# Attention in a two-layer decoder: the rotated queries' high and low parts stacked on the 128 rows of one tile, and the position queries projected before the plain ones

## The chip, the cores and the metric

The kernel runs on one core of a Trainium2 chip. The number that counts is the device time of one execution, in microseconds. TensorE (PE in the profile) multiplies matrices and writes to PSUM; its weight loads have a track of their own, PEld. VectorE is DVE, ScalarE is ACT, GpSimd is POOL, and SyncE (SP) issues most of the transfers from memory.

## The reference

Two layers over 256 positions of width 2048. Layer 0 is a gated short convolution and a squared-ReLU MLP; layer 1 is a latent attention and the same kind of MLP. Each sub-layer ends in a residual sum and a layer norm. The change lies in the attention. Cut to what matters:

```python
def apply_rope(x, cos, sin):
    x1, x2 = xf[..., :half], xf[..., half:]
    out = jnp.concatenate([x1 * cos - x2 * sin, x2 * cos + x1 * sin], axis=-1)

q = (rms_norm(x @ w_dq, q_norm_g) @ w_uq).reshape(bsz, seq, 16, 128 + 64)
q_nope, q_pe = q[..., :128], apply_rope(q[..., 128:], cos, sin)
s = (einsum("bqhd,bkhd->bhqk", qn, k_nope) + einsum("bqhr,bkr->bhqk", qp, k_pe)) * scale
p = softmax(where(mask, s, -inf))
```

There are 16 heads. A head's score is the sum of a plain product over 128 features and a position product over 64 rotated features; the rotated key k_pe is one for all heads.

## The kernel before

Activations lie with features on the 128 partitions and the 256 tokens along the free axis. To get nearly float32 accuracy from TensorE's faster type float32r, most operands are kept as a pair: a high part (the value rounded to float32r, made by ACT) and a low part (the rest, made by DVE with a subtraction); `split` makes both (L137), L139 being its ACT half and L140 its DVE half. A product of two such pairs takes three float32r matmuls: high by high, high by low, low by high. Weights stream from memory as units of 128x1024 floats into a ring of `raw` buffers, and each unit is split; `take` (L229) hands out the next units in the order of the list `stream` (L84 to L111) and prepares units ahead of their use.

In the attention the 16 heads are worked in four groups of four. `project(g, box)` (L1064) is a generator that makes the operands of one group: four key products (`ps_k`), four plain query products (`ps_q`), two position query products (`ps_p`, each for two heads, 64 rows per head), and two value products (`ps_v`). Each item ends in a `yield`. Group 0 is projected alone; after that the projections of group g are interleaved, three items at a time, with the attention steps of group g-1. `together(s)` (L1138) runs, in this order, the last part of head s-3, the middle part of head s-2 and the first part of head s. The first part of `attend` (L1098) makes the scores S and their softmax, the middle part transposes the probabilities (`tp`), the last part multiplies them with the values (`po`).

The scores are made in two spans, queries 0 to 127 against the first 128 keys and queries 128 to 255 against all 256 keys. The operands of the scores are plain float32 here: the plain product is L1107, the position product L1108. The position query tile holds two heads, 64 rows each, and `kpe` holds the rotated key twice, once with zeros in the lower 64 rows and once with zeros in the upper, so that a product over 128 rows takes only one head:

```python
nc.tensor.matmul(S[:, at:at + n], qn[:, tok], kn[:, :n], start=True, stop=False)
nc.tensor.matmul(S[:, at:at + n], qp[:, tok], kp[:, :n], start=False, stop=True)
```

`rope` (L983) rotates: a product with the cosines (L987), products with the sines in pieces of 32 rows that land on the rows 32 further up or down (L990, four for 128 rows), and a sum (L991).

Each engine runs its instructions in its own fixed order. That order is made when the program is built, by a scheduler that keeps dependences between instructions; a change in one place can so move instructions of neighbouring work.

Of the kernel before, what the change touches and what calls it, by code (L numbers as in the profile page):

```python
# [10 lines left out]
F32 = mybir.dt.float32  # L11
F32R = mybir.dt.float32r
AF = mybir.ActivationFunctionType
ALU = mybir.AluOpType
# [42 lines left out]
def trunk(ctx: ExitStack, tc: tile.TileContext, xT, vecs, lead, w_first, w_in, w_out, w_kv, w_q, w_uk, w_uv,  # L57
# [910 lines left out]
    with tc.tile_pool(name="att", bufs=1) as ap:  # L968
# [4 lines left out]
        mask_t = ap.tile([P, 3 * P], F32, name="mask_t")  # L973
        for t, source in ((cos_t, cosT), (sin_t, sinT), (mask_t, mask)):
            nc.sync.dma_start(t, source)
        kpe = ap.tile([P, 2, T], F32, name="kpe")
        nc.gpsimd.memset(kpe, 0.0)
        rc = ap.tile([P, 2], F32, name="rc")
        rk = ap.tile([P, T], F32, name="rk")
        sc = ap.tile([P, 2], F32, name="sc")  # L980
        nsc = ap.tile([P, 2], F32, name="nsc")

        def rope(dst, src, rows):  # L983

            a = tmp.tile([P, T], F32, tag="sq", name="ropea")
            b = tmp.tile([P, T], F32, tag="evac", name="ropeb")
            nc.vector.tensor_tensor(a[rows], src[rows], cos_t[rows], ALU.mult)  # L987
            for s in range(rows.start, rows.stop, 32):
                d = s ^ 32
                nc.vector.tensor_tensor(b[d:d + 32], src[s:s + 32], sin_t[s:s + 32], ALU.mult)  # L990
# [57 lines left out]
        def query_scale():  # L1048
# [7 lines left out]
        kq, vp = (act.tile([P, NC * W], F32, tag=a, name=f"kqv{a}") for a in ("a1", "a2"))  # L1056
        k2, q2, v2 = ([r[:, o:o + 1024].rearrange("p (j t) -> p j t", j=J) for o in (b, b + 1024)]
                      for r, b, J in ((kq, 0, 4), (kq, 2048, 4), (vp, 0, 2)))
        p2 = [vp[:, o:o + 512].rearrange("p (j t) -> p j t", j=2) for o in (2048, 2560)]
        pr2 = [vp[:, o:o + 3 * P] for o in (3072, 3456)]  # L1060

        with tc.tile_pool(name="att2", bufs=2) as a2, \
                tc.tile_pool(name="paux", bufs=1, space=PS) as paux:
            def project(g, box):  # L1064

                k4, q4, p4, v4 = (t[g % 2] for t in (k2, q2, p2, v2))
                box.update(k=k4, q=q4, p=p4, v=v4)
                w = take()
                for j in range(4):
                    ps = psum("ps_k")  # L1070
                    mm(ps, w, 4 * j, chl, NK)
                    nc.vector.tensor_tensor(k4[:, j, :], ps[:, :T], rk, ALU.mult)
                    yield
# [24 lines left out]
            def attend(h, box):  # L1098

                j = h % 4  # L1100
                qn, kn = box["q"][:, j, :], box["k"][:, j, :]
                qp, kp = box["p"][:, j // 2, :], kpe[:, h % 2, :]
                S = paux.tile([P, 512], F32, tag="S", name=f"S_{h}", bufs=2)
                spans = ((0, P), (P, T))
                for b, (at, n) in enumerate(spans):
                    tok = slice(b * P, (b + 1) * P)
                    nc.tensor.matmul(S[:, at:at + n], qn[:, tok], kn[:, :n], start=True, stop=False)  # L1107
                    nc.tensor.matmul(S[:, at:at + n], qp[:, tok], kp[:, :n], start=False, stop=True)  # L1108
# [3 lines left out]
                nc.vector.tensor_tensor(pr, S[:, :3 * P], mask_t, ALU.add)  # L1112
                for b, (at, n) in enumerate(spans):
                    nc.vector.tensor_reduce(mx[:, b:b + 1], pr[:, at:at + n], AX.X, ALU.max)
                nc.vector.tensor_tensor(mx, mx, nsc, ALU.mult)
                for b, (at, n) in enumerate(spans):
                    nc.scalar.activation(pr[:, at:at + n], pr[:, at:at + n], AF.Exp, bias=mx[:, b:b + 1],
                                         scale=sc[:, b:b + 1], accum_out=su[:, b:b + 1])
                nc.vector.reciprocal(su, su)
                for b, (at, n) in enumerate(spans):  # L1120
                    nc.vector.tensor_scalar(pr[:, at:at + n], pr[:, at:at + n], su[:, b:b + 1], None, ALU.mult)
                yield
                tp = paux.tile([P, 512], F32, tag="ta", name="tp")
                for n in range(3):
                    nc.tensor.transpose(tp[:, n * P:(n + 1) * P], pr[:, n * P:(n + 1) * P], id_t)
                pt = a2.tile([P, 3 * P], F32, tag="pt", name=f"pt_{h}")
# [250 lines left out]
```

## Time and profile before

| | |
|---|---|
| median of 3 runs | 1992.05 us (1992.02 to 1992.39) |
| the profiled execution | 1991.81 us |
| its span, first to last instruction | 1990.0 us |
| granted TensorE clock | 1.000 |
| attention: first key product to last product of a score step | about 1095 to 1227 us of the span |

A row of a timeline is: start, length, engine, line, operation, out<-in, form, count; lengths include the latency of one instruction, so the pace of a stream is the distance between starts. `xN` in a timeline row means that N neighbouring instructions were merged. A plain float32 matmul appears as two instructions (two passes), a float32r matmul as one; the profile prints the type of both as f32.

### The profile page before, as it was taken

The page shows a single profiled execution, that of the slowest core. Times are in us where ns is not written, and L with a number is a line of the kernel's source. Part 1 is how long each engine was busy: PE and PEld are TensorE (multiplying, and loading weights), DVE is VectorE, ACT ScalarE, POOL GpSimd, SP SyncE. Part 2 cuts the span into 40 slices and gives each one's busy share as a digit, 9 for nine tenths or more (in the row PEclk, how much of TensorE's full clock was granted, in tenths as well). Part 3 has the DMA queues.
Part 4 walks back from the last instruction along what each step waited for, and adds up shares of the span by engine and source line. Part 5 has one row for each costly group of instructions (what it writes and reads, how often), then busy time and mean ns, then how long its engine had stood idle before and what let it go on. Part 6 is the DMA issues. An engine that isn't in the chain of part 4 may idle for free.

```text
span 1990.0 us, 29545 instructions
## 1 busy us (share of the span) xinstructions
PE 1981.5 (100%) x11050; PEld 1729.1 (87%) x11050; DVE 1754.5 (88%) x2545; ACT 1277.3 (64%) x1873; POOL 20.6 (1%) x44
## 2 busy tenths in 40 slices
PE   9999999999999999999999999999999999999998
PEld 8888888988888888888889998898888888888886
DVE  8667667786999999999898988777799999999998
ACT  7444445585767767677656755557576776767764
POOL 0000000000000000000100000000000000000010
PEclk9999999999999999999999999999999999999999
DMA  9666666574566665666874543656366666666685
GB/s 344 212 189 189 190 188 188 179 238 131 197 205 209 203 203 190 209 210 197 270 263 149 181 139 122 203 183 191 118 202 203 198 211 206 197 201 202 213 241 171
DMA packets 110160, 394.72 MB, mean 198 GB/s; under 512 B 12224, under 2 KB 12992, under 8 KB 109504
## 3 DMA queue, kind: packets, MB, share of 16 engines
q1 hardware_dynamic: 106560, 383.79, 59.9%
q0 software_dynamic: 3312, 8.91, 1.9%
q8 instruction: 86, 1.41, 0.3%
q14 instruction: 58, 0.48, 0.1%
q10 hardware_dynamic: 144, 0.13, 0.0%
HBM read 384.40 MB, written 4.19 MB: 195 GB/s over the span
## 4 chain that ended last, share of the span: by engine, by line
PE 98%; ACT 1%; DVE 1%; issue 0%; DVEq 0%; ACTq 0%
PE ps_u L261 20%; PE ps_l L261 13%; PE ps_u L265 11%; PE ps L348 8%; PE ps L349 8%; PE ps L346 8%; PE ps_l L265 7%; PE ps_d L349 2%; PE ps_d L348 2%; PE ps_d L346 2%; PE ps_w L295 2%; PE ps_w L294 2%; PE ps_w L293 2%; PE ps_g L293 1%; PE ps_g L295 1%; PE ps_g L294 1%
## 5 line engine op out<-in xcount | busy, mean ns | idle before, releaser
L140 DVE TENSOR_TENSOR lo<-raw,hi 128x1024 fp32r<-128x1024 f32 x709 | 850.2, 1219 | 116.0 <-ACT hi L139 46.8
L139 ACT CAST hi<-raw 128x1024 fp32r<-128x1024 f32 x709 | 727.0, 1049 | 333.0 <-DVE raw L182 133.5
L261 PE MATMUL ps_u<-xhl,hi 128*128 128x512 f32 x1792 | 621.0, 393 | 0.1
L265 PE MATMUL ps_u<-xhl,lo 128*128 128x256 f32 x1792 | 485.5, 280 | 0.0
L261 PEld LDWEIGHTS ps_u<-xhl,hi 128*128 128x128 f32 x1792 | 329.1, 187 | 66.9 <-DVE fp L407 0.5
L265 PEld LDWEIGHTS ps_u<-xhl,lo 128*128 128x128 f32 x1792 | 338.1, 189 | 12.8
L261 PE MATMUL ps_l<-xhl_a,hi 128*128 128x512 f32 x704 | 244.1, 393 | 0.0
L265 PE MATMUL ps_l<-xhl_a,lo 128*128 128x256 f32 x704 | 195.4, 279 | 0.0
L261 PEld LDWEIGHTS ps_l<-xhl_a,hi 128*128 128x128 f32 x704 | 132.1, 188 | 29.9
L265 PEld LDWEIGHTS ps_l<-xhl_a,lo 128*128 128x128 f32 x704 | 131.9, 188 | 0.2
L177 DVE TENSOR_TENSOR raw_t<-raw,raw 128x1024 f32<-128x1024 f32 x100 | 121.8, 1218 | 1.0 <-DMA raw<-in_w2f_dram 1.0
L140 DVE TENSOR_TENSOR lo_t<-raw_t,hi_t 128x1024 fp32r<-128x1024 f32 x100 | 121.8, 1218 | 0.0
L406 ACT COPY t<-ps_u 128x256 f32<-128x256 f32 x112 | 41.5, 370 | 108.8 <-PE ps_u L265 108.4
L139 ACT CAST hi_t<-raw_t 128x1024 fp32r<-128x1024 f32 x100 | 105.2, 1052 | 0.0
L261 PE MATMUL ps_l<-z,hi 128*128 128x512 f32 x240 | 82.4, 391 | 0.0
L295 PE MATMUL ps_w<-xd,hi 128*128 128x258 f32 x256 | 72.7, 284 | 0.0
L294 PE MATMUL ps_w<-xd,lo 128*128 128x258 f32 x256 | 72.3, 282 | 0.0
L184 DVE TENSOR_TENSOR raw<-raw 128x512 f32<-128x512 f32 x100 | 69.2, 692 | 3.5
L293 PE MATMUL ps_w<-xd,hi 128*128 128x258 f32 x256 | 72.3, 282 | 0.0
L261 PE MATMUL ps_l<-oT,hi 128*128 128x512 f32 x208 | 71.3, 391 | 0.0
L407 DVE TENSOR_TENSOR fp<-ps_u,t 128x256 f32<-128x256 f32 x112 | 46.6, 416 | 27.9 <-ACT t L406 27.5
L140 DVE TENSOR_TENSOR t<-raw,t 128x512 fp32r<-128x512 f32 x100 | 68.4, 684 | 2.2 <-ACT t L139 2.2
(368 smaller groups left out, 3892.4 us busy)
## 6 DMA issues: line engine op xcount, KB each, us to landing
raw<-in_w_dram SPq DMA_DIRECT2D x312, 512.0 KB, 4.2
raw<-in_w2f_dram SPq DMA_DIRECT2D x200, 512.0 KB, 4.1
raw<-in_w_in_dram SPq DMA_DIRECT2D x88, 512.0 KB, 4.1
raw<-in_w_out_dram SPq DMA_DIRECT2D x32, 512.0 KB, 3.7
raw<-in_w_o_dram SPq DMA_DIRECT2D x32, 512.0 KB, 4.0
raw<-in_w_kv_dram SPq DMA_DIRECT2D x10, 512.0 KB, 5.1
raw<-in_w_q_dram SPq DMA_DIRECT2D x8, 512.0 KB, 4.1
raw<-in_w_uk_dram SPq DMA_DIRECT2D x8, 512.0 KB, 4.4
```

The lines of the kernel that those rows point to most:

```text
L139: nc.scalar.copy(hi, src)
L140: return nc.vector.tensor_tensor(lo, src, hi.bitcast(F32), ALU.subtract)
L177: nc.vector.tensor_tensor(t.rearrange(two, a=2), b12.unsqueeze(1).to_broadcast([P, 2, BW]), r1.rearrange(two, a=2), ALU.subtract)
L184: nc.vector.tensor_tensor(t4, b21, b12, ALU.subtract)
L261: nc.tensor.matmul(ps, w[blk // 8][0][:, blk % 8, :], x, start=first, stop=False)
L265: nc.tensor.matmul(ps[:, :T], w[blk // 8][1][:, blk % 8, :], x[:, :T], start=False, stop=last)
L293: nc.tensor.matmul(ps[:, :W], hi, x[k][:, :W], start=k == 0, stop=False)
L294: nc.tensor.matmul(ps[:, :W], lo, x[k][:, :W], start=False, stop=False)
L295: nc.tensor.matmul(ps[:, :W], hi, x[k][:, W:], start=False, stop=k == NC - 1)
L346: nc.tensor.matmul(ps, x[0], w[0], start=first, stop=False, skip_group_check=onto)
L348: nc.tensor.matmul(ps[:, at], x[0], w[1][:, at], start=False, stop=False, skip_group_check=onto)
L349: nc.tensor.matmul(ps, x[1], w[0], start=False, stop=last, skip_group_check=onto)
```

## The change

Three things change together.

First, the position product. The weights of the position queries are permuted on the host, so that the two heads of one `ps_p` tile alternate in blocks of 32 rows (first halves of both heads, then second halves). `rope` now rotates by halves of 64 rows: one cosine product, two sine products of 64 rows, one sum. A new function, `stacked`, turns the rotated tile into the operand of the scores: ACT writes the high part, 128x512, into both heads' halves of a tile `p`; DVE writes the low part into `plo`; and four transfers of 32 rows (32 KB each), issued by GpSimd, write the low parts over those rows of `p` that belong to the other head. Each head then has its 64 high rows and 64 low rows in one 128-row operand. The rotated key is repeated in the same pattern and split into `kph` and `kpl`. The position score is now two float32r matmuls, one with `kph` and one with `kpl`, in place of one float32 matmul. `plo` has one buffer; `p` has three.

Second, in `project` the two position query products come right after the key products, ahead of the plain queries, and the weight stream is reordered to match.

Third, buffers: the mask moves into the buffer that held the float32 position queries and is loaded later, and the transposed probabilities `pt` move there too; the zeroed `kpe` and its GpSimd memset go.

```diff
-        stream += halves(w_uk[g]) + halves(w_qn[g]) + halves(w_qp[g]) + halves(w_uv[g])
+        stream += halves(w_uk[g]) + halves(w_qp[g]) + halves(w_qn[g]) + halves(w_uv[g])
...
-        kpe = ap.tile([P, 2, T], F32, name="kpe")
-        nc.gpsimd.memset(kpe, 0.0)
+        kph = ap.tile([P, T], F32R, name="kph")
+        kpl = ap.tile([P, T], F32R, name="kpl")
...
-        def rope(dst, src, rows):
+        def rope(src):
 
             a = tmp.tile([P, T], F32, tag="sq", name="ropea")
             b = tmp.tile([P, T], F32, tag="evac", name="ropeb")
-            nc.vector.tensor_tensor(a[rows], src[rows], cos_t[rows], ALU.mult)
-            for s in range(rows.start, rows.stop, 32):
-                d = s ^ 32
-                nc.vector.tensor_tensor(b[d:d + 32], src[s:s + 32], sin_t[s:s + 32], ALU.mult)
-            nc.vector.tensor_tensor(dst[rows], a[rows], b[rows], ALU.add)
+            nc.vector.tensor_tensor(a, src, cos_t, ALU.mult)
+            for s, d in ((0, 64), (64, 0)):
+                nc.vector.tensor_tensor(b[d:d + 64], src[s:s + 64], sin_t[s:s + 64], ALU.mult)
+            nc.vector.tensor_tensor(a, a, b, ALU.add)
+            return a
...
-        for j in range(2):
-            rope(kpe[:, j, :], f, slice(64 * j, 64 * j + 64))
+        f = rope(f)
+        split(kph, kpl, f)
...
-        p2 = [vp[:, o:o + 512].rearrange("p (j t) -> p j t", j=2) for o in (2048, 2560)]
-        pr2 = [vp[:, o:o + 3 * P] for o in (3072, 3456)]
+        p2 = [ap.tile([P, 2, T], F32R, name=f"p{i}") for i in range(3)]
+        pr2, pt2 = ([vp[:, o:o + 3 * P] for o in (b, b + 3 * P)] for b in (2048, 2048 + 6 * P))
+        mask_t = vp[:, 2048 + 12 * P:2048 + 15 * P]
+        nc.sync.dma_start(mask_t, mask)
...
+            def stacked(dst, src):
+
+                nc.scalar.copy(dst, src.unsqueeze(1).to_broadcast([P, 2, T]))
+                lo = a2.tile([P, T], F32R, tag="plo", name="plo", bufs=1)
+                nc.vector.tensor_tensor(lo, src, dst[:, 0, :].bitcast(F32), ALU.subtract)
+                for s in range(0, P, 32):
+                    d = s ^ 32
+                    nc.gpsimd.dma_start(dst[d:d + 32, s // 32 % 2, :], lo[s:s + 32])
...
+                w = take(1)
+                for j in range(2):
+                    ps = psum("ps_p")
+                    mm(ps, w, 4 * j, qhl, NK)
+                    stacked(p4[j], rope(ps[:, :T]))
                     yield
...
-                w = take(1)
-                for j in range(2):
-                    ps = psum("ps_p")
-                    mm(ps, w, 4 * j, qhl, NK)
-                    rope(p4[:, j, :], ps[:, :T], slice(0, P))
-                    yield
...
-                qp, kp = box["p"][:, j // 2, :], kpe[:, h % 2, :]
+                qp = box["p"][j // 2][:, j % 2, :]
...
-                    nc.tensor.matmul(S[:, at:at + n], qp[:, tok], kp[:, :n], start=False, stop=True)
+                    nc.tensor.matmul(S[:, at:at + n], qp[:, tok], kph[:, :n], start=False, stop=False)
+                    nc.tensor.matmul(S[:, at:at + n], qp[:, tok], kpl[:, :n], start=False, stop=True)
```

Two places in the order of the engines carry the prediction. The first is TensorE at the scores of head 0, just behind the last value product of group 0. Before:

```order
L1107 MATMUL S_11150<-kqva_10884 128x128
L1108 MATMUL S_11150<-kpe,kqva_10885 128x128
L1107 MATMUL S_11150<-kqva_10884 128x256
L1108 MATMUL S_11150<-kpe,kqva_10885 128x256
L279 MATMUL ps_k<-lat,lo_10965 128x256
```

And with the change (L1118 is the plain product, L1119 and L1120 the two position products):

```order
L1118 MATMUL S_11158<-kqva_10878 128x128
L1119 MATMUL S_11158<-kph,p_10880 128x128
L1120 MATMUL S_11158<-kpl,p_10880 128x128
L1118 MATMUL S_11158<-kqva_10878 128x256
L1119 MATMUL S_11158<-kph,p_10880 128x256
L1120 MATMUL S_11158<-kpl,p_10880 128x256
L279 MATMUL ps_k<-lat,lo_10963 128x256
```

Each float32 position product has become two float32r products of the same shape; one of them streams 128 columns, the other 256.

The second is VectorE in the projections of group 0, from the last key copies on (`kqva<-ps_k` is a key copy, `nu` belongs to the layer norm of the residual, `lo` is the low part of a weight unit). Before, nine more rows follow these before the rotation begins:

```order
L1072 TENSOR_TENSOR kqva_10884<-ps_k,rk 128x256
L529 TENSOR_TENSOR nu<-xback,ab_10372 128x256 x2
L530 TENSOR_TENSOR nu<-nu,ab_10372 128x256 x2
L529 TENSOR_TENSOR nu<-xback,ab_10372 128x256
L140 TENSOR_TENSOR lo_11065<-raw_11062,hi_11064 128x1024
```

With the change it follows the key copies at once, and the low part of the second tile stands seven rows behind the low part of the first:

```order
L1083 TENSOR_TENSOR kqva_10878<-ps_k,rk 128x256 x2
L530 TENSOR_TENSOR nu<-nu,ab_10370 128x256
L529 TENSOR_TENSOR nu<-xback,ab_10370 128x256
L986 TENSOR_TENSOR ropea<-ps_p,cos_t 128x256
L988 TENSOR_TENSOR ropeb<-ps_p,sin_t 64x256 x2
L986 TENSOR_TENSOR ropea<-ps_p,cos_t 128x256
L989 TENSOR_TENSOR ropea<-ropea,ropeb 128x256
L988 TENSOR_TENSOR ropeb<-ps_p,sin_t 64x256 x2
L530 TENSOR_TENSOR nu<-nu,ab_10370 128x256
L1069 TENSOR_TENSOR plo<-ropea,p_10880 128x256
L989 TENSOR_TENSOR ropea<-ropea,ropeb 128x256
```

The rows that come next on the same engine:

```order
L529 TENSOR_TENSOR nu<-xback,ab_10370 128x256 x2
L530 TENSOR_TENSOR nu<-nu,ab_10370 128x256 x2
L140 TENSOR_TENSOR lo_11121<-raw_11118,hi_11120 128x1024
L140 TENSOR_TENSOR lo_11127<-raw_11124,hi_11126 128x1024
L1012 TENSOR_SCALAR rve<-rstat 128x2
L1069 TENSOR_TENSOR plo<-ropea,p_10881 128x256
```

The second `plo` writes the one buffer that the four transfers of the first still read, so VectorE waits there until these have landed, and everything below it in the list waits too. Between this row and the mask addition of head 0's scores (L1124) stand 16 further rows, three of them weight units.

More of the change, by code (lines that the diff above doesn't have):

```diff
@@ L972, in trunk @@
         sin_t = ap.tile([P, T], F32, name="sin_t")
-        mask_t = ap.tile([P, 3 * P], F32, name="mask_t")
-        for t, source in ((cos_t, cosT), (sin_t, sinT), (mask_t, mask)):
+        for t, source in ((cos_t, cosT), (sin_t, sinT)):
             nc.sync.dma_start(t, source)
-        kpe = ap.tile([P, 2, T], F32, name="kpe")
-        nc.gpsimd.memset(kpe, 0.0)
+        kph = ap.tile([P, T], F32R, name="kph")
+        kpl = ap.tile([P, T], F32R, name="kpl")
         rc = ap.tile([P, 2], F32, name="rc")
@@ L1058, in trunk @@
                       for r, b, J in ((kq, 0, 4), (kq, 2048, 4), (vp, 0, 2)))
-        p2 = [vp[:, o:o + 512].rearrange("p (j t) -> p j t", j=2) for o in (2048, 2560)]
-        pr2 = [vp[:, o:o + 3 * P] for o in (3072, 3456)]
+        p2 = [ap.tile([P, 2, T], F32R, name=f"p{i}") for i in range(3)]
+        pr2, pt2 = ([vp[:, o:o + 3 * P] for o in (b, b + 3 * P)] for b in (2048, 2048 + 6 * P))
+        mask_t = vp[:, 2048 + 12 * P:2048 + 15 * P]
+        nc.sync.dma_start(mask_t, mask)
         with tc.tile_pool(name="att2", bufs=2) as a2, \
                 tc.tile_pool(name="paux", bufs=1, space=PS) as paux:
+            def stacked(dst, src):
[5 more added lines that the diff above has]
+                    nc.gpsimd.dma_start(dst[d:d + 32, s // 32 % 2, :], lo[s:s + 32])
             def project(g, box):
-                k4, q4, p4, v4 = (t[g % 2] for t in (k2, q2, p2, v2))
+                k4, q4, v4 = (t[g % 2] for t in (k2, q2, v2))
+                p4 = [p2[(2 * g + j) % 3] for j in range(2)]
                 box.update(k=k4, q=q4, p=p4, v=v4)
@@ L1072, in project @@
                     nc.vector.tensor_tensor(k4[:, j, :], ps[:, :T], rk, ALU.mult)
+                    yield
+                w = take(1)
[3 more added lines that the diff above has]
+                    stacked(p4[j], rope(ps[:, :T]))
                     yield
@@ L1125, in attend @@
                     nc.tensor.transpose(tp[:, n * P:(n + 1) * P], pr[:, n * P:(n + 1) * P], id_t)
-                pt = a2.tile([P, 3 * P], F32, tag="pt", name=f"pt_{h}")
+                pt = pt2[h % 2]
                 nc.scalar.copy(pt, tp[:, :3 * P])
@@ L1327 @@
     dkv = a["kv_w_dkv"]
-    pe = dkv[:, RK:]
+    pe = np.repeat(dkv[:, RK:].reshape(D, 2, 1, 32), 2, axis=2).reshape(D, P)
     uq = a["mla_w_uq"][0].reshape(RK, H, 192)
@@ L1346 @@
         "w_out": _units(a["conv_w_out"][0]),
-        "w_kv": _units(np.concatenate([dkv, pe], axis=1)),
+        "w_kv": _units(np.concatenate([dkv[:, :RK], pe], axis=1)),
         "w_q": _units(a["mla_w_dq"][0]),
@@ L1351 @@
         "w_qn": _units(uq[:, :, :128].reshape(RK, -1)),
-        "w_qp": _units(uq[:, :, 128:].reshape(RK, -1)).reshape(4, 1, P, 1024),
+        "w_qp": _units(uq[:, :, 128:].reshape(RK, H // 2, 2, 2, 32).transpose(0, 1, 3, 2, 4).reshape(RK, -1)).reshape(4, 1, P, 1024),
         "w_o": _units(a["mla_w_o"][0]),
@@ L1358 @@
         "cosT": np.tile(cos, (4, 1)),
-        "sinT": np.tile(np.concatenate([sin, -sin]), (2, 1)),
+        "sinT": np.concatenate([sin, sin, -sin, -sin]),
         "mask": np.concatenate([tri, np.zeros((P, P), np.float32), tri], axis=1),
```

## The prediction

> **What bounds the kernel now.** First the page: busy time by engine, and the chain that ended last.
>
> ```profile
> span 1990.0 us, 29545 instructions
> PE 1981.5 (100%) x11050; PEld 1729.1 (87%) x11050; DVE 1754.5 (88%) x2545; ACT 1277.3 (64%) x1873; POOL 20.6 (1%) x44
> ...
> PE 98%; ACT 1%; DVE 1%; issue 0%; DVEq 0%; ACTq 0%
> ```
>
> TensorE is the chain, and busy in a profile does not yet mean that it streams at its pace. So the second view is what TensorE waited for in the whole execution, two rows in all:
>
> ```profile
> PE ps L1256 <- ACT umeans L1253: 1.6, 1, 1.6
> PE warm L423 <- DVE col L424: 1.1, 1, 1.1
> ```
>
> Neither lies in the attention. The third view, busy time by stretch there, says how near the others are (columns: PE, PEld, DVE, ACT, POOL busy, clock, DMA share, GB/s):
>
> ```profile
> 1095.00:1116.00 21.00, 21.00 (x156) 20.07 (x155) 20.68 (x46) 13.16 (x24) 0.00 (x0) 1.00 0.67 223
> 1116.00:1147.00 31.00, 31.00 (x222) 29.39 (x221) 30.72 (x75) 22.70 (x46) 0.00 (x0) 1.00 0.50 155
> 1147.00:1180.00 33.00, 33.00 (x237) 31.30 (x236) 28.46 (x73) 20.63 (x47) 0.00 (x0) 1.00 0.47 143
> 1180.00:1216.00 36.00, 36.00 (x238) 33.27 (x237) 30.61 (x83) 19.48 (x49) 0.00 (x0) 1.00 0.32 103
> ```
>
> VectorE works 98 to 99% of the first 52 us, so it has no room there, yet TensorE does not wait for it: it is late against itself, not against TensorE. The weights say why. The first output-projection unit (`w_o`) is requested at 1145.5 us and used at 1202.5 us:
>
> ```profile
> L150 SPq DMA_DIRECT2D raw<-in_w_o_dram x32: 327/328/328, 1145.5 to 1260.6; - x32
> ...
> L261 PE MATMUL ps_wo<-oT,hi x48: 391/394/586, 1202.5 to 1229.1; 128*128 128x512 f32 x48
> ```
>
> Work taken from VectorE or ACT is therefore worth nothing by itself. Only two things count: TensorE's own stream at the scores, and any wait that is long enough to reach it.
>
> **The scores on TensorE.** The timeline of TensorE at head 0:
>
> ```profile
> 1115.79 0.40 PE L349 MATMUL ps_v<-hi,lat 128*128 128x512 f32 x1
> 1116.03 0.39 PE L1107 MATMUL S<-kqva 128*128 128x128 f32 x2
> 1116.25 0.39 PE L1108 MATMUL S<-kpe,kqva 128*128 128x128 f32 x2
> 1116.47 0.60 PE L1107 MATMUL S<-kqva 128*128 128x256 f32 x2
> 1116.91 0.59 PE L1108 MATMUL S<-kpe,kqva 128*128 128x256 f32 x2
> ...
> 1117.46 0.28 PE L280 MATMUL ps_k<-lat,hi 128*128 128x256 f32 x1
> ...
> 1121.53 0.28 PE L281 MATMUL ps_k<-lat,hi 128*128 128x256 f32 x1
> ```
>
> Matmuls overlap, so I price by the distance between ends. The narrow position product (128 columns, two float32 passes) ends at 1116.64, 0.22 us behind the one ahead of it (1116.42); the wide one (256 columns) ends at 1117.50, 0.43 us behind 1117.07. Removed per head: 0.22 + 0.43 = 0.65 us.
>
> Added per head: two wide and two narrow float32r products. The wide price is in the trace: from 1117.46 to 1121.53 there are 34 steps of float32r products with 256 columns, 4.07 / 34 = 0.120 us each. Two cost 0.24 us where the float32 one cost 0.43.
>
> The narrow price is not in the trace: every float32r product of this kernel streams 256 columns or more. Three rows bound it. Lowest: half of the wide one, 0.060 us. Next: a product needs its own weight load, and the closest loads of the trace stand behind products of one column:
>
> ```profile
> 1107.12 0.54 PEld L1011 LDWEIGHTS rstat<-col,squares 128*128 128x128 f32 x4
> ...
> L1011 PEld LDWEIGHTS rstat<-col,squares x8: 186/192/192, 1080.4 to 1107.5; 128*128 128x128 f32 x8
> ```
>
> Four loads in 0.54 us, one lasting 0.19: (0.54 - 0.19) / 3 = 0.117 us apart. So 0.117 us if loads set the pace. Highest: as dear as the whole float32 product of that shape, 0.22 us; a reduced type should not cost more than the full one.
>
> Per head that gives 0.24 + 2 x 0.22 = 0.68 (plus 0.03 us), 0.24 + 2 x 0.117 = 0.474 (minus 0.18), or 0.24 + 2 x 0.060 = 0.36 (minus 0.29). Over 16 heads: plus 0.5, minus 2.8, minus 4.6 us. I take the upper end, plus 0.5. By shape the nearest row is the narrow float32 one, which works on the same tiles, the same 128 columns and four-byte operands; the wide row shows that float32r is fast on a long stream, and nothing here shows it on a short one.
>
> The Trainium skill, TensorE: Matmul & The Clock Gate, section Back-to-back issue gap, states about 81 ns per product with 128 columns in a stream of loads and products. By that the sum would be an estimated 16 x (0.24 + 0.162 - 0.65) = minus 4.0 us. The trace speaks against it: its loads are 117 ns apart with next to nothing streaming, and no row shows a shorter step.
>
> **The rotation, and the wait that comes with it.** VectorE, before:
>
> ```profile
> 1099.45 0.74 DVE L1072 TENSOR_TENSOR kqva<-ps_k,rk 128x256 f32<-128x256 f32 x2
> 1102.64 0.75 DVE L529 TENSOR_TENSOR nu<-xback,ab 128x256 f32<-128x256 f32 x2
> 1112.47 0.42 DVE L987 TENSOR_TENSOR ropea<-ps_p,cos_t 128x256 f32<-128x256 f32 x1
> 1113.25 1.72 DVE L990 TENSOR_TENSOR ropeb<-ps_p,sin_t 32x256 f32<-32x256 f32 x4
> 1116.48 2.36 DVE L140 TENSOR_TENSOR lo<-raw,hi 128x1024 fp32r<-128x1024 f32 x2
> 1118.87 0.56 DVE L1112 TENSOR_TENSOR kqva<-S,mask_t 128x384 f32<-128x384 f32 x1
> 1125.26 0.54 DVE L1121 TENSOR_SCALAR kqva<-kqva,su 128x128 f32<-128x128 f32 x2
> ```
>
> An operation of 128x256 takes a step of 0.34 us (two in 0.75, one 0.41), a sine piece 0.43 (four in 1.72; I give the 64-row piece the same), a weight unit 1.15 (two in 2.36, one 1.21). A rotation goes from 0.34 + 4 x 0.43 + 0.34 = 2.40 to 0.34 + 2 x 0.43 + 2 x 0.34 = 1.88 us with its low part: VectorE gains 0.5 us per tile, 4 us over eight, and about 1 us at the key. Nothing of it reaches the end. ACT gets eight casts of 128x512. The nearest row, a cast of that shape, takes 0.62 us, 5 us over the eight; ACT is 63 to 73% busy in the first two stretches:
>
> ```profile
> 1060.14 0.62 ACT L139 CAST sq<-SQ 128x512 fp32r<-128x512 f32 x1 [0.52 <-DVE SQ L477]
> ```
>
> The new wait is VectorE's, at the second `plo` of each group. For group 0 I lay the new order onto these steps. From 1099.45 us: nine operations and one weight unit, 9 x 0.34 + 1.15 = 4.2, rotation from 1103.7; four operations and four sine pieces, 3.1, first `plo` from 1106.8 to 1107.2; five operations, two weight units and a small one, 4.1: the second `plo` is due at 1111.2. The four transfers are issued from 1107.2 on. The price of an issue and of a landing, from the POOL timeline and the table of transfers:
>
> ```profile
> 994.55 1.65 POOL L933 DMA_DIRECT2D xback<-parked  x3 [5.66 <-ACT hi L139]
> ...
> xback<-parked POOLq DMA_DIRECT2D x4, 512.0 KB, 6.3
> ...
> out_dram<-acc SPq DMA_DIRECT2D x8, 256.0 KB, 2.6
> ```
>
> Issues 0.55 us apart, so the fourth at 1108.8; landing 2.6 to 6.3 us later, 1111.4 to 1115.1. VectorE waits 0.2 to 3.9 us; the middle, 4.4 us of landing, gives 2.0. Head 0's score products need these transfers only at 1116.25, so TensorE itself does not wait for them even at the late end.
>
> What is late next: the softmax of head 0. Behind the second `plo` come about eight operations, three units and seven small steps, 7.1 us with its own, so the mask addition starts at 1118.3 plus the wait, against 1118.87 before. The scaled probabilities were ready 6.9 us later, at 1125.80, and the same kinds of rows lie in between; now 1125.2 plus the wait. They are due when TensorE transposes them:
>
> ```profile
> 1127.27 0.49 PE L1125 MATMUL tp<-id_t,kqva 128*128 128x128 f32 x3
> ```
>
> So TensorE waits for whatever exceeds 2.1 us: nothing in the middle case, 1.8 us at the late end. I take 0. Head 2's transposition, whose softmax follows the second `plo` of group 1, had far more room, from 1135.83 to 1143.07 us:
>
> ```profile
> 1135.28 0.55 DVE L1121 TENSOR_SCALAR kqva<-kqva,su 128x128 f32<-128x128 f32 x2
> ...
> 1143.07 0.49 PE L1125 MATMUL tp<-id_t,kqva 128*128 128x128 f32 x3
> ```
>
> The Trainium skill, DMA: Bandwidth & Descriptors, section Anatomy of one DMA, gives 2.0 us plus bytes over 436 KB per us for a transfer from GpSimd, an estimated 2.1 us for 32 KB: the wait would vanish. No transfer of that size is among the POOL rows, so no run shown here tells.
>
> **Moved and left out.** A group's 24 position products (two items of 12) move ahead of its 48 plain ones, the same products on the same operands: no time on TensorE. The mask load now waits for the last product that reads the buffer it moves into, and SP's later loads of `w_q` queue behind it:
>
> ```profile
> L349 PE MATMUL ps_d<-hi,h1a x32: 389/389/396, 1000.3 to 1040.0; 128*128 128x512 f32 x32
> ...
> 1028.66 24.39 SPq L150 DMA_DIRECT2D raw<-in_w_q_dram  x7
> ...
> 1063.81 2.93 ACT L139 CAST hi<-raw 128x1024 fp32r<-128x1024 f32 x3
> ```
>
> It is held to 1040 us; the units behind it are first cast at 1063.81, so some 20 us hide it. The memset on POOL had no follower. All at nothing.
>
> **Sum.** Plus 0.5 on the scores, 0 for waits: 1991.81 + 0.5 = 1992.3 us for the profiled execution, whose time is 0.24 below the median; against 1992.05 that is 1992.6 us.
>
> **Rivals.** Load-paced narrow products: minus 2.8, 1989.3 us. For it the loads at 117 ns; against it that nothing says a short float32r stream keeps its pace. Still too small to be told from no change; this kernel's measurement tells about 0.2%, 4 us.
>
> Fully fast narrow products at 0.060 us: minus 4.6, 1987.5 us. Against it the same loads.
>
> Late transfers, the slower side: one mechanism at one place, the second `plo` of group 0, priced by the slowest rows of the POOL queue:
>
> ```profile
> 966.35 0.88 POOL L673 DMA_DIRECT2D acc<-sums  x1 [4.92 <-DVE raw L184]
> ...
> acc<-sums POOLq DMA_DIRECT2D x12, 256.0 KB, 6.6
> ```
>
> Issues 0.88 us apart and 6.6 us to land put the fourth at 1107.2 + 2.6 + 6.6 = 1116.4. VectorE waits 5.2 us, head 0's transposition is 3.1 us late, and the total is 1992.05 + 0.5 + 3.1 = 1995.7 us. It begins to cost when the landing passes 1113.3 us, and is over 0.2% from 1116.7. For it: VectorE is full there, and these two figures are what this queue shows. Against it: those rows move eight times as much and add to what they overwrite.
>
> **How the numbers follow.** Forecast 0.53; load-paced 0.31; fully fast 0.07; late transfers 0.09. Faster by over 0.2% is the third case, 0.07; slower is the part of the last that lands after 1116.7, 0.05; the rest, 0.88, within. The range takes in the load-paced case (with 0.5 for rounding) and the late end of the forecast, 1992.6 + 1.8, reaching 0.6 further into the last case: 1988.8 to 1995.0 us.
>
> **What would show it.** In the changed profile, the end of a narrow position product against the one ahead: 0.22 confirms, 0.12 or 0.06 the rivals. The wait of VectorE at `plo`, and whether TensorE's waits gain a row at `tp`. TensorE instructions: the position rows keep their count of 64, now as 32 and 32 single products. I am wrong if TensorE's time at the scores stays and the total moves by more than 2 us, or if a wait appears outside the attention.

## The result

The changed kernel takes 1989.38 us (median of 22 runs, 1988.5 to 1991.23) where the kernel before takes 1992.03 us (22 runs, 1991.4 to 1994.01). The ratio is 0.9986 with a 95% interval of 0.998 to 0.9992: it is 2.65 us faster, 0.13%. The prediction took 0.2%, 4 us, for the least that this kernel's measurement can tell; with 22 runs of each kernel the interval is 1.2 us to either side, so the gain is real. The forecast of 1992.6 us was wrong. The rival that it held for less likely, narrow products at the distance of their weight loads, 1989.3 us, is the time that came.

The profiled execution of the changed kernel, its span and the busy time of the engines:

```profile
span 1987.1 us, 29631 instructions
PE 1978.5 (100%) x11050; PEld 1726.5 (87%) x11050; DVE 1749.8 (88%) x2534; ACT 1281.5 (64%) x1882; POOL 35.9 (2%) x75
```

The span is 2.9 us shorter, TensorE's busy time 3.0 us. VectorE loses 4.7 us, ACT gains 4.2, POOL 15.3 for the issues of the transfers. The waits of TensorE, in the same columns as before (total, times, longest):

```profile
PE ps L1268 <- ACT umeans L1265: 1.6, 1, 1.6
PE warm L423 <- DVE col L424: 1.1, 1, 1.1
```

They are the same two rows, with new line numbers. So no wait went away and none came: TensorE's own stream became shorter. The busy time by stretch, before and then after the change, shows that it did so in the attention:

```profile
1095.00:1227.00 132.00, 132.00 (x913) 123.81 (x912) 117.60 (x290) 82.34 (x180) 0.00 (x0) 1.00 0.46 147
1230.00:2000.00 770.00, 752.64 (x4013) 647.03 (x4011) 700.21 (x929) 507.40 (x705) 7.87 (x9) 1.00 0.61 193
```

```profile
1095.00:1224.00 129.00, 129.00 (x912) 121.43 (x911) 112.44 (x281) 85.72 (x186) 15.82 (x32) 1.00 0.49 155
1230.00:2000.00 770.00, 749.64 (x3997) 644.52 (x3995) 697.36 (x920) 504.25 (x698) 7.90 (x9) 1.00 0.60 193
```

The attention's stretch holds the same number of product records in 129 us as before in 132 (913 and 912), at a granted clock of 1.00 both times. From 1230 us to the end TensorE has 3.0 us less to do, because 16 more products are behind it by then.

TensorE's timeline at head 0 is where the prediction had said to look:

```profile
1115.65 0.40 PE L349 MATMUL ps_v<-hi,lat 128*128 128x512 f32 x1
1115.89 0.39 PE L1118 MATMUL S<-kqva 128*128 128x128 f32 x2
1116.03 0.30 PE L1119 MATMUL S<-kph,p 128*128 128x128 f32 x1
1116.17 0.28 PE L1120 MATMUL S<-kpl,p 128*128 128x128 f32 x1
1116.28 0.65 PE L1118 MATMUL S<-kqva 128*128 128x256 f32 x2
1116.58 0.47 PE L1119 MATMUL S<-kph,p 128*128 128x256 f32 x1
1116.88 0.29 PE L1120 MATMUL S<-kpl,p 128*128 128x256 f32 x1
```

By ends (start plus length), the six products run from 1116.05 to 1117.17: 1.12 us. The four of before ran from 1116.19 to 1117.50, 1.31 us. That is 0.19 us per head and 3.0 us over 16 heads, all of the gain. The other heads show the same: from the start of a head's first product to the end of its last are 1.47 us at all sixteen before, and 1.27 to 1.29 after. Inside it, the wide pair (L1119 and L1120 with 256 columns) ends at 1117.17, 0.24 us behind the wide plain product at 1116.93, as costed. The narrow pair needs care. Its two ends, 1116.33 and 1116.45, are 0.05 and 0.12 us behind the product ahead, but the wide plain product then ends 0.48 us later, where it took 0.43 before. Together, from the narrow plain product's end (1116.28) to the wide plain product's (1116.93), 0.65 us; less the 0.43 of the plain product, the two narrow ones cost 0.22 us. The one float32 product that they replace cost 0.22 us too.

The weight loads of these rows:

```profile
1116.00 0.19 PEld L1119 LDWEIGHTS S<-kph,p 128*128 128x128 f32 x1
1116.11 0.19 PEld L1120 LDWEIGHTS S<-kpl,p 128*128 128x128 f32 x1
1116.22 0.30 PEld L1118 LDWEIGHTS S<-kqva 128*128 128x128 f32 x2
```

They start 0.11 us apart, and 0.11 us is the price of a narrow product. The products of one column in the prediction had their loads 0.117 us apart, with next to nothing to stream, so the columns need not be what sets this price. That it is the load is the likely reading, no more: every product in these traces has its own load of 128x128, and another fixed price per product would look the same.

The other new things, VectorE around the rotation in group 0:

```profile
1106.43 0.42 DVE L1069 TENSOR_TENSOR plo<-ropea,p 128x256 fp32r<-128x256 f32 x1
...
1110.83 0.16 DVE L1012 TENSOR_SCALAR rve<-rstat 128x2 f32<-128x2 f32 x1
1110.90 0.42 DVE L1069 TENSOR_TENSOR plo<-ropea,p 128x256 fp32r<-128x256 f32 x1
...
1124.04 0.54 DVE L1133 TENSOR_SCALAR kqva<-kqva,su 128x128 f32<-128x128 f32 x2
```

The second `plo` starts at 1110.90, right behind the small operation ahead of it: in group 0, where the prediction had placed the wait, VectorE does not wait. The first four transfers had landed by then, as the view of the tile `plo` says of the POOL rows from 1107 to 1109 us:

```profile
L1072 POOL DMA_DIRECT2D p<-plo x4: 493/503/521, 1107.4 to 1108.9; - x4
...
DMA to landing us min/median/max: 1.7/1.7/1.8
```

The same view over the whole execution (durations are minimum, median, maximum, in ns) gives all transfers and all eight low parts, and what VectorE was idle for before them:

```profile
L1072 POOL DMA_DIRECT2D p<-plo x32: 489/492/597, 1107.4 to 1193.6; - x32
L1069 DVE TENSOR_TENSOR plo<-ropea,p x8: 416/426/426, 1106.4 to 1190.9; 128x256 fp32r<-128x256 f32 x8
...
  DMA p<-plo: 1.3, 1
...
DMA to landing us min/median/max: 1.7/3.3/5.6
```

Transfers land 1.7 to 5.6 us after their issue, and VectorE waited for them once, 1.3 us, ahead of the second low part of group 2.

### The profile page after: what moved, and what is told of

It is laid out like the page before. It is cut to its first block, busy times and chain, and to the rows that moved or that the text cites. A ratio compares the mean times of both kernels' runs of the same rounds, so it can differ in the third digit from the quotient of the medians.

```text
span 1987.1 us, 29631 instructions
## 1 busy us (share of the span) xinstructions
PE 1978.5 (100%) x11050; PEld 1726.5 (87%) x11050; DVE 1749.8 (88%) x2534; ACT 1281.5 (64%) x1882; POOL 35.9 (2%) x75
## 4 chain that ended last, share of the span: by engine, by line
PE 97%; DVE 1%; ACT 1%; DMA 1%; issue 1%; SPq 0%; DVEq 0%; ACTq 0%
PE ps_u L261 21%; PE ps_l L261 13%; PE ps_u L265 11%; PE ps L348 8%; PE ps L349 8%; PE ps L346 8%; PE ps_l L265 7%; PE ps_d L348 2%; PE ps_d L346 2%; PE ps_d L349 2%; PE ps_w L295 1%; PE ps_w L293 1%; PE ps_w L294 1%; PE ps_g L295 1%; PE ps_g L293 1%; PE ps_g L294 1%
## 5 line engine op out<-in xcount | busy, mean ns | idle before, releaser
L265 PEld LDWEIGHTS ps_u<-xhl,lo 128*128 128x128 f32 x1792 | 338.1, 189 | 12.8
```

What stands on the lines that cost most here:

```text
L265: nc.tensor.matmul(ps[:, :T], w[blk // 8][1][:, blk % 8, :], x[:, :T], start=False, stop=last)
```

## The experiments

Two theories compete. **Load-paced**: a narrow float32r product costs 0.11 us, the distance of two weight loads, the narrow span gains nothing, the wide span gains 0.19 us per head, and the transfers stay hidden. Against it stand those in which the gain has another source: the new order of the projections, VectorE's relief, or narrow products that are fast by themselves. All ratios are to the kernel before, measured on the same chip as the run. The changes tested are so small that the time alone often can't decide; then the distance per head in the timeline does.

**The wide span alone.** The narrow position product goes back to one float32 product, on the same stacked queries, with a float32 key that VectorE adds up once:

```diff
+        kpf = vp[:, 2048 + 15 * P:2048 + 16 * P]
+        nc.vector.tensor_tensor(kpf, kph[:, :P].bitcast(F32), kpl[:, :P].bitcast(F32), ALU.add)
...
+                    if n == P:
+                        nc.tensor.matmul(S[:, at:at + n], qp[:, tok].bitcast(F32), kpf[:, :n], start=False, stop=True)
+                        continue
```

> The change with its position product of the 128-column span as one float32 product of the stacked queries with a float32 key (its result stays right); the 256-column span keeps the two float32r products. Load-paced theory (a short float32r product costs one weight load, 0.11 us, so two of them cost what the one float32 product costs, 0.22): the gain lies in the wide span alone, so this is as fast as the change, 2.6 us under the kernel before, 1989.4 us, within 0.5. Stream theory (a short product costs its columns, 0.06): 16 x 0.10 = 1.6 us of the gain is lost, 1991.0. Theory that the gain comes from the new order or from VectorE's relief: as fast as the change as well.

Measured: 1989.65 us (11 runs), ratio 0.9988 [0.9979, 0.9997]; span 1987.1 us, the same as that of the whole change. Its TensorE timeline at head 0, the narrow position product and the wide plain product behind it:

```profile
1116.30 0.39 PE L1122 MATMUL S<-kqva,p 128*128 128x128 f32 x2
1116.52 0.60 PE L1120 MATMUL S<-kqva 128*128 128x256 f32 x2
```

From the end of the narrow float32 product (1116.69) to that of the wide plain one (1117.12) are 0.43 us. The 0.05 us by which the plain product was late behind a float32r pair are gone, and the narrow product takes them back itself. All sixteen heads take 1.27 to 1.29 us, as with the whole change. The time alone would not exclude the stream theory's 1991.0 us, since the interval reaches 1991.5; the timeline does. The wide span carries the whole gain.

**The narrow span alone.** The converse: float32r keys of 128 columns, a float32 key of 256 for the wide span.

```diff
-        split(kph, kpl, f)
+        split(kph, kpl, f[:, :P])
+        nc.scalar.copy(kpf, f)
...
+                    if n == T:
+                        nc.tensor.matmul(S[:, at:at + n], qp[:, tok].bitcast(F32), kpf[:, :n], start=False, stop=True)
+                        continue
```

> The converse: the 256-column span's position product is one float32 product of the stacked queries with a float32 key, the 128-column span keeps its two float32r products. Load-paced theory: nothing is left of the gain on TensorE, 16 x 0.19 = 3.1 us slower than the change, within 0.5 us of the kernel before, 1992.0. Stream theory: 1.6 us under the kernel before, 1990.4. Order or VectorE theory: as fast as the change, 1989.4.

Measured: 1992.19 us (11 runs), ratio 1.0 [0.9991, 1.0009]. All sixteen heads take 1.47 or 1.48 us, as in the kernel before: two narrow float32r products are worth the one float32 product that they replace. (The time alone leaves 1.8 us open to either side.) With the experiment before, this closes the sum: 0 from the narrow span, the gain from the wide. And since this kernel keeps the new order, the new rotation and the transfers, and gains nothing, none of these is the source.

**More narrow products.** To measure the disputed price by itself, the low part's narrow product is issued twice more per head, 32 products in all. The scores are then wrong by a small term.

```diff
-                    nc.tensor.matmul(S[:, at:at + n], qp[:, tok], kpl[:, :n], start=False, stop=True)
+                    nc.tensor.matmul(S[:, at:at + n], qp[:, tok], kpl[:, :n], start=False, stop=n == T)
+                    for i in range(2 if n == P else 0):
+                        nc.tensor.matmul(S[:, at:at + n], qp[:, tok], kpl[:, :n], start=False, stop=i == 1)
```

> The change with two more products of the stacked queries with the low key per head in the 128-column span, 32 in all (the scores are then wrong by a small term). Load-paced theory: 0.11 us each, 3.6 us more than the change, 1993.0. Stream theory: 0.06 each, 1.9 us more, 1991.3. The price taken in the prediction, 0.22 each: 7.0 us more, 1996.4.

Measured: 1994.69 us (11 runs), ratio 1.0014 [1.0006, 1.0023], 5.3 us over the change. That is more than the load-paced theory expected, and less than 0.22 us each would give; the interval, 1993.3 to 1996.7 us, excludes the 1993.0 of the first and not the 1996.4 of the second. The timeline of TensorE at a later head:

```profile
1122.46 0.28 PE L1120 MATMUL S<-kpl,p 128*128 128x128 f32 x1
1122.58 0.39 PE L1122 MATMUL S<-kpl,p 128*128 128x128 f32 x2
1122.80 0.65 PE L1118 MATMUL S<-kqva 128*128 128x256 f32 x2
```

And that of its weight loads there:

```profile
1122.40 0.19 PEld L1120 LDWEIGHTS S<-kpl,p 128*128 128x128 f32 x1
1122.52 0.30 PEld L1122 LDWEIGHTS S<-kpl,p 128*128 128x128 f32 x2
1122.74 0.30 PEld L1118 LDWEIGHTS S<-kqva 128*128 128x128 f32 x2
```

The two extra products end at 1122.97, 0.23 us behind the one ahead at 1122.74: 0.11 us each, 3.6 us over 32, as the load-paced theory has it, and the loads start 0.11 to 0.12 us apart on average over the piece (the row with x2 holds two). All sixteen heads show it: 1.49 to 1.52 us, about 0.22 over the change. What is left lies beside the products. The profiled execution is the slowest of the eleven, 1996.38 us, and its span of 1994.6 us is 7.5 over that of the change. There TensorE's waits have three rows that the change has not, 2.0 us in all:

```profile
PE mu0p L461 <- ACT kqva L1106: 0.9, 1, 0.9
PE po L1145 <- DVE oT L412: 0.9, 1, 0.9
PE ps_u L261 <- DVE fp L407: 0.2, 1, 0.2
```

The products and these rows make 5.6 of the 7.5 us. The other 1.9 are not placed, and why so small an addition brings these waits stays open.

**The order alone.** The kernel before, with the position queries projected second and their weights to match, and nothing else.

```diff
-        stream += halves(w_uk[g]) + halves(w_qn[g]) + halves(w_qp[g]) + halves(w_uv[g])
+        stream += halves(w_uk[g]) + halves(w_qp[g]) + halves(w_qn[g]) + halves(w_uv[g])
...
+                w = take(1)
+                for j in range(2):
+                    ps = psum("ps_p")
+                    mm(ps, w, 4 * j, qhl, NK)
+                    rope(p4[:, j, :], ps[:, :T], slice(0, P))
+                    yield
...
```

> The kernel before with nothing but the position queries projected second, as in the change; the products, the rotation in pieces of 32 rows and the buffers stay. If the gain is that of the products: no difference to the kernel before, 1992.0 within 0.4. If the order brings it: 1989.4.

Measured: 1991.95 us (11 runs), ratio 1.0001 [0.9992, 1.001]. The order alone is not the source of the gain.

**The old place.** The change, with the position queries projected third again, so that rotation, cast and transfers come later.

```diff
-        stream += halves(w_uk[g]) + halves(w_qp[g]) + halves(w_qn[g]) + halves(w_uv[g])
+        stream += halves(w_uk[g]) + halves(w_qn[g]) + halves(w_qp[g]) + halves(w_uv[g])
...
-                w = take(1)
-                for j in range(2):
-                    ps = psum("ps_p")
-                    mm(ps, w, 4 * j, qhl, NK)
-                    stacked(p4[j], rope(ps[:, :T]))
-                    yield
...
                 for _ in range(4):
                     ln.normal(next(todo))
+                w = take(1)
+                for j in range(2):
+                    ps = psum("ps_p")
+                    mm(ps, w, 4 * j, qhl, NK)
+                    stacked(p4[j], rope(ps[:, :T]))
+                    yield
```

> The change with its position queries projected third again, behind the plain queries, as in the kernel before; the stacking, the transfers and the products stay. Theory that the new place is what hides the transfers: in group 0 the position products then end near 1110 us, the first low part follows near 1113, four transfers 0.5 us apart and 3.3 us to land end near 1118, and head 0's position product, due at 1116.0, waits about 2 us on TensorE; its softmax then comes late too: 2 to 4 us more than the change, 1991.4 to 1993.4. Theory that the place does not matter, since TensorE works at the same products either way: 1989.4.

Measured: 1992.3 us (11 runs), ratio 1.0001 [0.9992, 1.001], 2.9 us over the change. The gain is given back. Its waits of TensorE hold two rows that the change has not:

```profile
PE S L1119 <- ACT kqva L1106: 0.9, 1, 0.9
PE S L1119 <- issue: 0.4, 1, 0.4
```

One row names ACT, but the trace points to a transfer. POOL's issues, and then TensorE, at head 0:

```profile
1114.41 2.02 POOL L1072 DMA_DIRECT2D p<-plo  x4 [116.07 <-DVE ropeb L988]
```

```profile
1118.03 0.30 PE L1119 MATMUL S<-kph,p 128*128 128x128 f32 x1 [0.85 <-ACT kqva L1106]
```

`stacked` fills head 0's rows with the first and the third of the four transfers. The third is issued at 1115.4 and lands 2.5 us later by this run's trace, at 1117.9; the product that reads these rows starts at 1118.03. The second row is the same thing at head 4: the third transfer is issued at 1141.2, lands 3.4 us later, at 1144.6, and the product starts at 1144.64. In the changed kernel the first issue stands at 1107.4, seven microseconds earlier, and all four have landed by 1110.7. The two rows make 1.3 us; the spans of the two profiled executions, 1989.5 and 1987.1 us, differ by 2.4. The rest has no wait row, and is not placed.

**Late transfers.** In the change, each set of four transfers is issued three times over with the same data, so that they land late.

```diff
-                for s in range(0, P, 32):
+                for s in 3 * list(range(0, P, 32)):
```

> The change with each group of four transfers issued three times over (same rows, same data, the result stays right), so that the second low part of a group has to wait for twelve. Theory of the prediction's slower rival (VectorE waits in its queue and head 0's softmax behind it has about 2.2 us of room): the twelfth transfer of group 0 lands near 1107.4 + 11 x 0.5 + 3.3 = 1116.2, VectorE waits about 5.3 us, TensorE 3 us, and the later groups up to 1 us each: 3 to 6 us more than the change, 1992.4 to 1995.4. Theory that VectorE's waits never reach TensorE because its weights are split 10 us and more ahead: 1989.4.

Measured: 2002.91 us (5 runs), ratio 1.0053 [1.004, 1.0065], 13.5 us over the change. All expectations were too small. The waits of TensorE and the one of VectorE that matters:

```profile
PE S L1119 <- DMA p<-plo: 8.4, 4, 3.5
...
PE po L1143 <- DVE oT L412: 0.9, 2, 0.5
PE ps_g L261 <- ACT hi L139: 0.4, 1, 0.4
```

```profile
DVE plo L1069 <- DMA p<-plo: 16.5, 4, 5.8
```

VectorE does wait at `plo`, 16.5 us, as the late-transfers rival had it. But TensorE's list has no row for `tp`, the transposition through which that rival let the wait reach TensorE. TensorE waits, four times, in the score products that read the transferred rows themselves: at heads 0 and 8, the first tile of a group, and at heads 10 and 14, the second tile, whose transfers are issued behind VectorE's wait. So where VectorE's wait counts, it is by these transfers and not by the softmax. The first of these waits also shows an extra price. The windows of this kernel around it (columns as before, the clock is third from the right), and its timeline:

```profile
1120.00:1122.00 2.00, 1.88 (x7) 1.70 (x8) 1.56 (x2) 0.39 (x1) 0.62 (x2) 0.58 0.00 0
1122.00:1124.00 2.00, 2.00 (x13) 2.00 (x12) 1.92 (x4) 0.00 (x0) 1.82 (x4) 0.57 0.61 160
1124.00:1126.00 2.00, 2.00 (x19) 2.00 (x18) 1.37 (x5) 1.16 (x5) 0.00 (x0) 1.00 1.04 264
```

```profile
1120.12 0.33 PE L1119 MATMUL S<-kph,p 128*128 128x128 f32 x1 [3.46 <-DMA p<-plo]
...
1122.06 0.41 PE L280 MATMUL ps_k<-lat,hi 128*128 128x256 f32 x1
1122.27 0.41 PE L281 MATMUL ps_k<-lat,hi 128*128 128x256 f32 x1
```

After 3.46 us without a product, TensorE was granted 0.58 and 0.57 of its clock for close to 4 us, and products of 256 columns came 0.21 us apart instead of 0.12. By the two timelines, the products from this one to the tenth key product took 3.64 us (1120.12 to 1123.76) and in the change 2.05 (1116.03 to 1118.08): 1.6 us lost. With it, the waits of 9.7 us make 11.3 of the 12.8 us between the spans of the profiled executions, 1999.9 and 1987.1; the remaining 1.5 are not placed.

**The low part in place.** Here the low part is written over the rotated tile, so that the second no longer needs the buffer that the transfers of the first read:

```diff
-                lo = a2.tile([P, T], F32R, tag="plo", name="plo", bufs=1)
+                lo = src.bitcast(F32R)
```

> The change without the separate buffer for the low part: the subtraction writes over the rotated tile, which has two buffers, so the second low part of a group no longer waits for the transfers of the first. VectorE's wait there, 1.3 us in all in the profile of the change, goes. If that wait is hidden, as the rows say: 1989.4 within 0.4. If it costs: up to 1.3 us less.

Measured: 1989.03 us (11 runs), ratio 0.9985 [0.9976, 0.9994], 0.35 us under the change. That is no difference these runs can tell. VectorE's list has no wait for the transfers any more, and the span is 1987.2 us against 1987.1: the 1.3 us at `plo` were hidden.

**One load for two products.** If the narrow pair is paced by weight loads, then merging it should free it: both products use the same weights, the queries of the first span. The high and low keys go into one tile, and one product of 256 columns writes the two results to the two ends of the bank; VectorE adds the second to the first after the mask.

```diff
-        kph = ap.tile([P, T], F32R, name="kph")
-        kpl = ap.tile([P, T], F32R, name="kpl")
+        khl = ap.tile([P, 2, T], F32R, name="khl")
+        kph, kpl = khl[:, 0, :], khl[:, 1, :]
...
+                ends = S.rearrange("p (a c) -> p a c", c=P)[:, ::3, :]
+                nc.tensor.matmul(ends, qp[:, :P], khl[:, :, :P], start=True, stop=False)
+                nc.tensor.matmul(S[:, :P], qn[:, :P], kn[:, :P], start=False, stop=True)
...
+                nc.vector.tensor_tensor(pr[:, :P], pr[:, :P], S[:, 3 * P:], ALU.add)
```

> The change with the two narrow position products made one of 256 columns: the first 128 columns of the high and of the low key stream behind one weight load into columns 0 to 127 and 384 to 511 of the score tile, the plain product is added to the first, and VectorE adds the last 128 columns after the mask (one more operation of 128x128 per head). Load-paced theory: 0.22 us become 0.12, 16 x 0.10 = 1.6 us less than the change, 1987.8, if VectorE's extra step of about 0.2 us per head stays hidden. If short products cost their columns: no gain, 1989.4. If the extra step reaches TensorE in the last heads, whose room is 0.7 to 1.5 us: between the two.

Measured: 1987.76 us (10 runs), ratio 0.9977 [0.9967, 0.9986]. It is 4.35 us faster than the kernel before and 1.6 us faster than the change. TensorE at head 0:

```profile
1116.07 0.39 PE L349 MATMUL ps_v<-hi,lat 128*128 128x512 f32 x1
1116.30 0.28 PE L1117 MATMUL S<-khl,p 128*128 128x256 f32 x1
...
1117.19 0.28 PE L1123 MATMUL S<-khl,p 128*128 128x256 f32 x1
```

The merged product ends 0.12 us behind the one ahead, where the pair cost 0.22; the five products of a head run from 1116.46 to 1117.47, 1.01 us instead of 1.12. Over 16 heads that is 1.8 us, and 1.6 came. The addition that VectorE gets in each head brings no wait at the scores; TensorE's list has one new row, 0.3 us on VectorE, in the MLP behind the attention. One load for two products fits, and so would any price that comes once per product, or a float32r stream that is slow only below 256 columns; the one-column products, 0.117 us apart, make the last unneeded, but no run here separates the three.

## Why the prediction was wrong, point by point

**What bounds the kernel** held. TensorE is the chain in both kernels, with the same two waits. VectorE's 4.7 us less and ACT's 4.2 us more moved nothing that shows, as costed.

**The wide products** held: 0.24 us for the pair against 0.43, in the change and with the wide span alone.

**The narrow products** are the step that failed. The prediction bounded a narrow float32r product at 0.060, 0.117 and 0.22 us, and took 0.22, "the narrow float32 one, which works on the same tiles". The runs show 0.11 us: loads 0.11 us apart in the change, 0.11 us for each product added, and a narrow span that alone changes nothing. Two at 0.22 made plus 0.5 us of what is minus 3.0. The mechanism was in the prediction, with its price from the loads of the one-column products, 0.117 us apart; the choice went by the likeness of shape to a float32 product. That product makes two passes, each with its own load. Its loads before, at head 0:

```profile
1116.14 0.30 PEld L1108 LDWEIGHTS S<-kpe,kqva 128*128 128x128 f32 x2
```

Two loads, one of them 0.19 us long, in 0.30 us are 0.11 us apart. The prediction's own bound, that a reduced type should not cost more than the full one, is to be taken per pass: a float32r product is one pass, so its upper end was half of 0.22, 0.11 us, and the load row said 0.117. Bound and load row agreed on about 0.11. The reading that missed it took a float32 product for one product. That the two agree may be chance: float32 takes 0.43 us for 256 columns and half of that for 128, so its narrow pass may be as long as its stream needs, and not as its load does.

**The fully fast rival** fell for two separate products, which come 0.11 us apart. Its price, 0.060 us per 128 columns, is right where one load serves both: the merged product takes 0.12 us.

**The estimate of minus 4.0 us** by the Trainium skill, TensorE: Matmul & The Clock Gate, section Back-to-back issue gap, has the right sign and is too large for the pair. The trace differs: the loads of the narrow pair start 0.11 us apart, not 0.081, and the pair costs 0.22 us, not 0.162.

**The rotation and the transfers** held in sum and not in place. The first low part was forecast for 1106.8 and ran at 1106.43, the second was due at 1111.2 and ran at 1110.90; the fourth transfer was issued at about 1108.9 (1107.4 and three issues of 0.49), against 1108.8. The wait of 0.2 to 3.9 us at that place, taken as 2.0, was not there. The step that failed there is the landing, taken as 4.4 us from transfers of 256 and 512 KB: the four of group 0 land in 1.7 to 1.8 us, by 1110.7, ahead of the second low part. Over all 32 the median is 3.3 us. The formula of the Trainium skill, DMA: Bandwidth & Descriptors, section Anatomy of one DMA, estimated 2.1 us and by it no wait: in group 0 the trace agrees, with 1.7 to 1.8 us and no wait, while over all 32 transfers 2.1 us lies near the lower end (1.7 at the least) and is not the usual value. The room behind it was right: probabilities ready at 1124.58, against a forecast of 1125.2 with no wait, and no row of TensorE at `tp`.

**The late-transfers rival** named the wrong place. It let late transfers reach TensorE through VectorE and head 0's softmax. When they were made late, TensorE stopped at the products that read the transferred rows. The prediction had looked at these products only with the changed order, where the transfers land in time; from the old place they do not, and the gain is given back. The order move was costed at nothing, which is right alone (1991.95 us); beside the transfers it is worth 2.9 us, 1.3 of them seen as waits.

**The load of the mask, the weight queue, the memset**: no TensorE wait names any of them.

The time lies inside the predicted range, which had taken in the load-paced case, and within the 0.2% to either side to which it gave a chance of 0.88. That is the width of the range and not the forecast's mechanism: the forecast had the scores get slower, and they got faster.

## What to carry to other kernels

Count passes, not products: a float32 product is two passes with two weight loads, so half its price bounded the float32r product of the same shape from above in these runs. At 128 columns that bound, 0.11 us, is the price; at 256 it is not, 0.215 us against 0.120. Where two short products share their weights, put their moving operands side by side and stream them behind one load. A reordering that is worth nothing by itself can be what hides a new transfer, so try the parts of a change together with what they are there to cover, as well as alone.

## What the runs showed that was not expected

The price of a short product does not show in its own row. Here it ended 0.05 us behind its predecessor, and another 0.05 us appeared at the float32 product behind it. Only the distance across the whole group, 0.65 us, tells it.

A wait of 3.46 us on TensorE cost about half as much again, since the clock granted after it was 0.58 and 0.57 until about 1123.8 us. The Trainium skill, TensorE: Matmul & The Clock Gate, Part 1: The HAM clock gate, says that an idle window of about 3.4 us halves the clock, and that some 3.4 us of work restore it. This run agrees with both lengths, an idle stretch of 3.46 us and 3.6 us of slow products behind it; the clock that its windows show is 0.57, a little over half. Three shorter waits of the same kernel, the longest 1.93 us, were followed by full pace, with a granted clock of 1.00:

```profile
1220.89 0.30 PE L1119 MATMUL S<-kph,p 128*128 128x128 f32 x1 [1.93 <-DMA p<-plo]
```

The releaser that a wait row names can be the wrong one. With the old place, one row says ACT and the other nothing; the third transfer's landing, at 1117.9 and 1144.6 us, less than 0.2 us ahead of each product, says that it was the transfer.
